# Seven products of quarters in the second feed-forward's gate and up blocks

## The chip, the cores and the metric

One core of a Trainium2 chip runs the whole layer in one launch. The engines that matter are TensorE (matmuls; PE in the profile, its weight loads PEld), VectorE (DVE), ScalarE (ACT), GpSimd (POOL) and SyncE (SP), whose queue issues the loads of weights. The metric is the device time of one execution in microseconds, as the median of several executions of the same program.

## The reference, cut to what matters

```
def swiglu(x, w_gate, w_up, w_down):
    return (jax.nn.silu(x @ w_gate) * (x @ w_up)) @ w_down

h = swiglu(rms_norm(x, ff1_pre_g), ff1_w_gate, ff1_w_up, ff1_w_down)
x = x + 0.5 * rms_norm(h, ff1_post_g)
...  # mixer: differential attention heads and state-space groups, then w_out
x = x + rms_norm(mixed, mix_post_g)
h = swiglu(rms_norm(x, ff2_pre_g), ff2_w_gate, ff2_w_up, ff2_w_down)
x = x + 0.5 * rms_norm(h, ff2_post_g)
```

There are 512 tokens of 1024 channels; the hidden width of both feed-forwards is 2816, that is 22 blocks of 128. All inputs and the output are float32.

## The kernel before, in words

Every float32 product is computed as three matmuls of rounded numbers (fp32r): each operand is split into a high part (a cast on ACT) and a low part (a subtraction on DVE), and `mm3` multiplies high by high, high by low and low by high into the same PSUM tile. So a block of 128 hidden channels times 512 tokens over 1024 channels is 8 x 3 = 24 matmuls of 512 columns.

`Normed` (line 208) holds the normed input, transposed to channels by tokens, as two `hi` and two `lo` tiles. Its method `tile(t)` treats 128 tokens: sums of squares on ACT, scaling on DVE into `xs`, four transposes of each half on PE into `ps_xn`, and from there the cast and the subtraction.

The second feed-forward begins with `gate_up_start` (line 348): blocks 0 and 1 of gate and up, four products in the four `acc` banks of PSUM. `halves` runs them in two passes, tokens 0 to 255 and then tokens 256 to 511, with matmuls of 256 columns; between the products of the first pass it lets in the transposes of token tiles 2 and 3. Their weights are split ahead (`w_lead`, the low part on POOL). `gate_up` (line 353) then does blocks 0 and 1's `finish` and goes through blocks 2 to 21: for gate and up each, one weight block is loaded (512 KB, SP queue), split (`wh` by ACT, line 154; `wl` by DVE, line 155), and multiplied (`ps_gu`, lines 188 to 190). `finish` makes silu of the gate on ACT (`sg`, L361), multiplies on DVE (`hf`, L363), and splits the product at once into high and low `h` (L365 and L366). `out_block` (line 316) multiplies h by the down weights in two passes of 512 output channels, with h as the stationary operand.

Buffers come from pools with a fixed number of slots: 3 for raw weights, 4 for each of `wh` and `wl`, 15 pages of 8 KB a partition in the heap, 2 for rows of gains, 6 for `scratch`, and 8 PSUM banks (4 `acc`, 2 `m`, 2 `sc`). An instruction that needs a slot waits for the last reader of an older tile. Inside the block `with tc.manual_schedule(engines={PE})` TensorE's order is the order of the program; the order of the other engines is made at build time by a planner that simulates the program and lets each engine take the first ready instruction in program order. `after(ins)` puts the instructions of ins's engine that are traced inside it behind ins. `behind` (line 354) keeps the splits of the next weights on ACT and DVE behind the last norm work of the input.

Of the kernel before, what the change touches and what calls it, by code (L numbers as in the profile page):

```python
# [8 lines left out]
F32 = mybir.dt.float32  # L9
F32R = mybir.dt.float32r  # L10
# [3 lines left out]
ALU = mybir.AluOpType  # L14
# [28 lines left out]
HEAD_PADS = (2.05, 0.85, 1.0, 0.6)  # L43
GLU_COST = (0.8, 0.65, 1.0)
GT = "m"


@with_exitstack
def hybrid_layer(
# [21 lines left out]
    def page(shape, dtype=F32, name="page"):  # L71
        return heap.tile(shape, dtype, tag="page", name=name)
# [6 lines left out]
    def scratch(shape, dtype=F32, name="scratch"):  # L79
        return tmp.tile(shape, dtype, tag="scratch", name=name)  # L80
# [70 lines left out]

    def split(raw, wh, wl, eng=dve, rows=None):
        if rows is None:
            act.copy(wh, raw)  # L154
# [51 lines left out]
        return s  # L206

    class Normed:
        def __init__(self, gain, g=None):
            self.g = g if g is not None else gain_row(gain, DM, "pre_g")  # L210
            self.hi = [page([P, 4, SEQ], F32R, "xn_hi") for _ in range(2)]
            self.lo = [page([P, 4, SEQ], F32R, "xn_lo") for _ in range(2)]

        def tile(self, t, hold=(), pads=()):
            xt = x_sb[t]
            ss = [sum_sq(xt[:, h * 512:(h + 1) * 512], 1.0 / 32, f"pre{h}") for h in range(2)]
            self.last_sq = sum_sq.ins
            with after(*hold[0:1]):
                r = rsqrt_of(ss, EPS, "pre")
            xs = []  # L220
            for h in range(2):
                xs.append(scratch([P, 512], F32, "xs"))
                cs = slice(h * 512, (h + 1) * 512)
                with after(*hold[1:]):
                    self.last = dve.scalar_tensor_tensor(xs[h], xt[:, cs], r, self.g[:, cs], ALU.mult, ALU.mult).ins
            yield
            for h in range(2):
                ps = bank("m" if h else "sc", "ps_xn")
                for k in range(4):
# [7 lines left out]
                self.lo_ins = dve.tensor_tensor(self.lo[h][:, :, t * P:(t + 1) * P], pv, hi.bitcast(F32),  # L237
                                                ALU.subtract).ins

        def get(self, k, a=0, b=SEQ):  # L240
            return self.hi[k // 4][:, k % 4, a:b], self.lo[k // 4][:, k % 4, a:b]
# [67 lines left out]
    def drain(gen):  # L309
        while True:  # L310
            try:
                next(gen)
            except StopIteration as e:
                return e.value

    def out_block(lhs, w, nf, last, gain, half, finished, hooks={}, order0=None, tags0=("acc",) * NT, gains_of=None):
# [19 lines left out]
        steps = row_steps(lhs, w, nf, 0, order0 or outer(nf, 4), done0, hooks, tags0, gains_of=gains_of)  # L336
# [5 lines left out]
        yield drain(row_steps(lhs, w, nf, 512, outer(nf, last), done1, hooks, norm_at=norm_at, gains_of=gains_of))  # L342
# [10 lines left out]
    def gate_up(xn, first, w_gate, w_up, tick=None):  # L353
# [17 lines left out]
        for f in range(lead, NF):  # L371
# [8 lines left out]
            if f >= 3:  # L380
                behind.clear()
        return lambda f: (h[f // 2][:, f % 2, 0, :], h[f // 2][:, f % 2, 1, :])


    rows_left = []
# [688 lines left out]
    for _ in background:  # L1074
        pass

    def next_norm(gain, lead):
        box = {}

        def start():  # L1080
            box["n"] = Normed(gain)
            box["w"] = lead()

        return box, start, lambda t: box["n"].tile(t)
# [43 lines left out]
            for _ in range((1, 4, 1)[GLU_ORDER[:n].count(c)]):  # L1128
                yield next(parts[int(c)])

    box, start, fin = next_norm(ff2_pre_g, lambda: gate_up_lead(ff2_w_gate, ff2_w_up))
# [13 lines left out]
    with tc.manual_schedule(engines={mybir.EngineType.PE}):  # L1145
# [46 lines left out]
```

## Time and profile before

| | us |
|---|---|
| median of 3 runs | 957.99 (957.38 to 958.18) |
| profiled execution, its own time | 962.16 |
| its span, first to last instruction | 960.4 |
| PE busy in the span | 946.3 (99%) |
| DVE busy | 470.5 (49%) |
| ACT busy | 333.0 (35%) |
| POOL busy | 78.0 (8%) |

Matmuls are pipelined, so a busy PE is not PE at its peak: the pace is read from the starts of successive matmuls. The granted clock of TensorE is 1.00 in all 40 slices but the last stretch, which is 2.4 GHz.

### The profile page before, as it was taken

How to read it: one execution, taken by the hardware profiler on the slowest of the kernel's cores; microseconds unless marked ns; L12 is line 12 of the kernel's file. 1: busy time of each engine (PE TensorE's matmuls, PEld its weight loads, DVE VectorE, ACT ScalarE, POOL GpSimd, SP SyncE). 2: the span in 40 equal slices, each digit the busy share in tenths (PEclk: the TensorE clock that was granted, in tenths of full speed). 3: DMA queues.
4: the chain of work that ended last, by engine and by line, in shares of the span. 5: the costliest groups of instructions: out<-in, count | busy, mean ns of one | idle time of the engine just before them, and what ended most of it. 6: DMA issues, size and time to landing. Idle time of an engine off the chain costs nothing.

```text
span 960.4 us, 12657 instructions
## 1 busy us (share of the span) xinstructions
PE 946.3 (99%) x4956; PEld 785.7 (82%) x4956; DVE 470.5 (49%) x919; ACT 333.0 (35%) x558; POOL 78.0 (8%) x157
## 2 busy tenths in 40 slices
PE   9999999999999999999999999999999999999997
PEld 5988878888888888988777778988888888888886
DVE  5599987433322324739578658333333333322323
ACT  5422333232311233523657565323223232222311
POOL 2100000000000031110122334000000000000000
PEclk9999999999999999999999999999999999999999
DMA  6636453533223264753612142333333333323212
GB/s 197 182 94 171 126 161 114 156 88 105 93 90 109 88 214 158 176 132 100 111 44 89 44 125 75 109 93 104 88 110 88 99 99 90 108 88 105 93 44 88
DMA packets 145981, 106.85 MB, mean 111 GB/s; under 512 B 15585, under 2 KB 126721, under 8 KB 145154
## 3 DMA queue, kind: packets, MB, share of 16 engines
q1 hardware_dynamic: 143776, 100.93, 35.9%
q0 software_dynamic: 992, 3.02, 1.0%
q10 hardware_dynamic: 1154, 2.10, 0.6%
q8 instruction: 39, 0.64, 0.3%
q14 instruction: 20, 0.16, 0.1%
HBM read 97.15 MB, written 8.88 MB: 110 GB/s over the span
## 4 chain that ended last, share of the span: by engine, by line
PE 47%; DVE 3%; DMA 2%; issue 1%; ACT 1%; POOL 1%; DVEq 0%; POOLq 0%; SPq 0%; ACTq 0%
PE ps_gu L188 8%; PE ps_gu L189 8%; PE ps_gu L190 8%; PE acc L188 5%; PE acc L190 5%; PE acc L189 5%; DMA om<-om_d 1%; PE ps_o L958 1%; DMA mm<-kd 1%; DMA raw<-in_ff_w_gate_dram 1%; PE ps_sc L929 0%; PE ps_k L188 0%; PE ps_y L817 0%; PE ps_k L190 0%; PE ps_xn L230 0%
## 5 line engine op out<-in xcount | busy, mean ns | idle before, releaser
L154 ACT CAST wh<-raw 128x1024 fp32r<-128x1024 f32 x146 | 153.2, 1052 | 468.7 <-issue 165.3
L155 DVE TENSOR_TENSOR wl<-raw,wh 128x1024 fp32r<-128x1024 f32 x146 | 180.4, 1239 | 276.1 <-ACT wh L154 253.8
L188 PE MATMUL ps_gu<-xn_hi,wh 128*128 128x512 f32 (+1 forms) x696 | 265.4, 382 | 0.0
L189 PE MATMUL ps_gu<-xn_lo,wh 128*128 128x512 f32 (+1 forms) x696 | 265.0, 381 | 0.0
L190 PE MATMUL ps_gu<-xn_hi,wl 128*128 128x512 f32 (+1 forms) x696 | 264.9, 381 | 0.0
L190 PEld LDWEIGHTS ps_gu<-xn_hi,wl 128*128 128x128 f32 x696 | 130.8, 188 | 25.3 <-issue 0.2
L188 PEld LDWEIGHTS ps_gu<-xn_hi,wh 128*128 128x128 f32 x696 | 130.7, 188 | 25.3 <-issue 0.6
L189 PEld LDWEIGHTS ps_gu<-xn_lo,wh 128*128 128x128 f32 x696 | 130.9, 188 | 24.5
L189 PE MATMUL acc<-wl,h 128*128 128x512 f32 x352 | 136.8, 389 | 0.0
L188 PE MATMUL acc<-wh,h 128*128 128x512 f32 x352 | 136.7, 389 | 0.0
L190 PE MATMUL acc<-wh,h 128*128 128x512 f32 x352 | 136.3, 389 | 0.0
L363 DVE TENSOR_TENSOR hf<-sg,ps_gu 128x512 f32<-128x512 f32 x44 | 30.3, 688 | 109.1 <-PE ps_gu L190 108.3
L190 PEld LDWEIGHTS acc<-wh,h 128*128 128x128 f32 x352 | 66.1, 188 | 13.8
L189 PEld LDWEIGHTS acc<-wl,h 128*128 128x128 f32 x352 | 66.1, 188 | 13.7
L188 PEld LDWEIGHTS acc<-wh,h 128*128 128x128 f32 x352 | 66.1, 188 | 13.5
L325 POOL TENSOR_SCALAR ss<-ss_post 128x1 f32<-128x1 f32 x12 | 2.6, 213 | 544.2 <-ACT junk_post L205 544.2
L365 ACT CAST h<-hf 128x512 fp32r<-128x512 f32 x44 | 27.3, 621 | 11.2 <-DVE hf L363 10.5
L366 DVE TENSOR_TENSOR h<-hf,h 128x512 fp32r<-128x512 f32 x44 | 30.2, 686 | 1.4 <-ACT h L365 1.4
L205 ACT ACTIVATE junk_post<-acc 128x512 bf16<-128x512 f32 x24 | 14.3, 594 | 37.8 <-PE acc L190 37.5
L361 ACT ACTIVATE sg<-ps_gu 128x512 f32<-128x512 f32 x44 | 25.9, 589 | 1.8 <-PE ps_gu L190 1.8
L492 DVE TENSOR_TENSOR pslots<-itca,a 128x128 f32<-128x128 f32 (+2 forms) x48 | 20.2, 466 | 8.6 <-DMA kd<-pslots 8.2
L155 POOL TENSOR_TENSOR w_lead<-raw,w_lead 128x1024 fp32r<-128x1024 f32 x8 | 19.6, 2455 | 21.1 <-ACT w_lead L154 21.1
(284 smaller groups left out, 1130.8 us busy)
## 6 DMA issues: line engine op xcount, KB each, us to landing
raw<-in_ff_w_gate_dram SPq DMA_DIRECT2D x44, 512.0 KB, 3.9
raw<-in_ff_w_up_dram SPq DMA_DIRECT2D x44, 512.0 KB, 4.0
raw<-in_ff_w_down_dram SPq DMA_DIRECT2D x44, 512.0 KB, 3.3
raw<-in_w_in_dram SPq DMA_DIRECT2D x16, 512.0 KB, 4.6
raw<-in_w_out_dram SPq DMA_DIRECT2D x8, 512.0 KB, 3.3
im_d<-itca SPq DMA_DIRECT2D x4, 512.0 KB, 3.4
om_d<-taps SPq DMA_DIRECT2D x4, 512.0 KB, 3.9
im<-im_d SPq DMA_DIRECT2D x2, 1024.0 KB, 10.0
```

What stands on the lines that cost most here:

```text
L154: act.copy(wh, raw)
L155: eng.tensor_tensor(wl, raw, wh.bitcast(F32), ALU.subtract)
L188: pe.matmul(ps, a[0], b[0], start=start, stop=False)
L189: pe.matmul(ps, a[0], b[1], start=False, stop=False)
L190: last_mm[:] = [pe.matmul(ps, a[1], b[0], start=False, stop=stop).ins]
L205: sum_sq.ins = act.activation(into, src, AF.Square, scale=scale, accum_out=s).ins
L361: act.activation(sg, ps_g, AF.Silu)
L363: dve.tensor_tensor(hf, sg, ps_u, ALU.mult)
L365: act.copy(hi, hf)
L366: dve.tensor_tensor(lo, hf, hi.bitcast(F32), ALU.subtract)
L492: dve.tensor_tensor(t[ri], a, by, ALU.mult)
L958: pe.matmul(po[:, os], at[:, kb * P:(kb + 1) * P], A.v[:, kb, h * VD:(h + 1) * VD], start=(kb == 0), stop=(kb == i), skip_group_check=True)
```

## The change

For gate and up each, blocks f and f + 10 (f from 2 to 11) are computed together as a product of 2 x 2 quarters: a pair's 256 hidden channels, the 1024 input channels and the 512 tokens are all halved, and eight products of quarters become seven (a Winograd form of Strassen's scheme). A quarter product has 4 steps over channels of 3 matmuls of 256 columns. `Normed` keeps a third, unrounded copy of the transposed input (`raw`, copied by ACT), and `combine` makes four combinations of its quarters on DVE, each split into high and low. `prepared` loads the two weight blocks of a job, splits the first as it is (parts 1 and 2), makes four combinations of quarters in place on DVE, and splits what results (parts 6 and 3, part 7, parts 5 and 4). A `Job` owns two PSUM banks, each of them holding two quarters of 256 columns. Between the products, ACT copies partial sums out of PSUM (`p1`, `u2`, `p5`, `u3`) and DVE adds them to other quarters in PSUM. There are 20 jobs. h is kept whole (`keep`), and `Held` splits it when the down products need it, once in each of the two passes.

The products are now traced inside the block in which PE's order is the program's.

```diff
     class Normed:
-        def __init__(self, gain, g=None):
+        def __init__(self, gain, g=None, keep=False):
+            self.raw = [page([P, 4, SEQ], F32, "xn_raw") for _ in range(2)] if keep else None
+            self.late = []
...
+            if t >= 2:
+                self.flush()
...
                 self.hi_ins = act.copy(hi, pv).ins
+                if self.raw:
+                    self.late.append(lambda o=self.raw[h][:, :, t * P:(t + 1) * P], i=pv: act.copy(o, i))
...
+        def combine(self):
+            self.flush()
+            (b11, b12), (b21, b22) = ([r[:, :, 0:256], r[:, :, 256:512]] for r in self.raw)
+            out, self.cut_ins = {}, []
+            def parts(name, v):
+                both = page([P, 2, 4, 256], F32R, "xt")
+                self.cut_ins.append(act.copy(both[:, 0], v).ins)
+                dve.tensor_tensor(both[:, 1], v, both[:, 0].bitcast(F32), ALU.subtract)
+                out[name] = both[:, 0], both[:, 1]
+            dve.tensor_tensor(b11, b12, b11, ALU.subtract)
+            dve.tensor_tensor(b12, b22, b12, ALU.subtract)
+            dve.tensor_tensor(b22, b22, b11, ALU.subtract)
+            parts(6, b22)
+            parts(7, b12)
+            parts(5, b11)
+            dve.tensor_tensor(b21, b21, b22, ALU.subtract)
+            parts(4, b21)
...
+    class Held:
+        def __call__(self, f):
+            if f // 2 not in self.cut:
+                self.cut[f // 2] = both = page([P, 2, 2, SEQ], F32R, "h_cut")
+                for n in range(2):
+                    hv = self.at[f // 2 * 2 + n]
+                    act.copy(both[:, n, 0], hv)
+                    dve.tensor_tensor(both[:, n, 1], hv, both[:, n, 0].bitcast(F32), ALU.subtract)
...
+    def gate_up_seven(xn, first_two, w_gate, w_up):
...
+        def prepared(w, f0, f1):
+            def raw():
+                turn[0] += 1
+                if RAWPAGE and turn[0] % 4 == 0:
+                    return gains.tile([P, KD, P], F32, tag="gain", name="raw")
+                return ring.tile([P, KD, P], F32, tag="raw", name="raw", bufs=3)
...
+            by[1], by[2] = parts(ra)
+            s3 = scratch([P, 4, P], F32, "s3")
+            dve.tensor_tensor(s3, a11, a21, ALU.subtract)
+            dve.tensor_tensor(a21, a21, a22, ALU.add)
+            dve.tensor_tensor(a11, a21, a11, ALU.subtract)
+            dve.tensor_tensor(a12, a12, a11, ALU.subtract)
+            by[6], by[3] = parts(ra)
+            h3, l3 = (scratch([P, 4, P], F32R, f"s3{c}") for c in "hl")
+            split(s3, h3, l3)
+            by[7] = h3, l3
+            by[5], by[4] = parts(rb)
...
+            def product(self, m):
+                ps = {1: self.c11, 2: self.c11, 3: self.c12, 6: self.c12, 4: self.c21, 7: self.c21, 5: self.c22}[m]
+                (wh, wl), (xh, xl) = self.by[m], xt[m]
+                for k in range(4):
+                    for i, (a, b) in enumerate(((wh, xh), (wh, xl), (wl, xh))):
+                        pe.matmul(ps, a[:, k], b[:, k], start=(m in (1, 7) and k == i == 0), ...
...
+        job, nxt = Job(0), None
+        xt.update(xn.combine())
+        with after(xn.cut_ins[CUT], *job.s_ins):
+            for f in range(lead):
+                keep(f, gate(first_two[2 * f][0]), first_two[2 * f + 1][0])
+        first(job)      # product 1 into c11; ACT copies it to p1
+        second(job)     # product 6 into c12; DVE adds p1; ACT copies the sum to u2
+        for n, (w, f0, f1) in enumerate(jobs):
+            nxt = Job(n + 1) if n + 1 < len(jobs) else None
+            job.product(7)
+            job.product(5)
+            add(job.c21, job.c21, u2)
+            act.copy(u3, job.c21)
+            act.copy(p5, job.c22)
+            add(job.c22, job.c22, u3)
+            if nxt:
+                first(nxt)
...
+            job.product(2)
+            job.product(3)
+            add(job.c12, job.c12, p5)
+            job.product(4)
+            if nxt:
+                second(nxt)
+            if n % 2 == 0:
+                sgs = [gate(b) for b in job.banks]
+            else:
+                for f, sg, b in zip((f0, f1), sgs, job.banks):
+                    keep(f, sg, b)
...
-    lhs = gate_up(box["n"], lhs, ff2_w_gate, ff2_w_up)
+        lhs = gate_up_seven(box["n"], lhs, ff2_w_gate, ff2_w_up)
```

A job's seven products run on PE as 7, 5, (1 of the next job), 2, 3, 4, (6 of the next job).

## Rows read from the trace of the kernel before

**Rows 1.** The page, part 1: busy us, share of the span, instructions.
```profile
PE 946.3 (99%) x4956; PEld 785.7 (82%) x4956; DVE 470.5 (49%) x919; ACT 333.0 (35%) x558; POOL 78.0 (8%) x157
```

**Rows 2.** Stretches: lead blocks' products, blocks 2 to 21, first pass of the down products.
```profile
core 0: us, PE busy (x) PEld busy (x) DVE busy (x) ACT busy (x) POOL busy (x), PEclk, DMA share, GB/s
592.01:616.77 24.76, 24.76 (x209) 24.75 (x208) 14.19 (x20) 11.24 (x19) 2.15 (x4) 1.00 0.36 107
616.77:834.40 217.63, 217.63 (x962) 180.25 (x961) 73.70 (x79) 62.14 (x79) 0.00 (x0) 1.00 0.32 95
834.40:896.00 61.60, 61.60 (x273) 51.05 (x272) 17.45 (x17) 15.71 (x21) 0.85 (x4) 1.00 0.26 86
```

**Rows 3.** Timeline of PE, start and duration in us, at three stage borders.
```profile
605.25 0.28 PE L188 MATMUL ps_gu<-xn_hi,w_lead 128*128 128x256 f32 x1
...
616.77 0.40 PE L188 MATMUL ps_gu<-xn_hi,wh 128*128 128x512 f32 x1
...
834.40 0.39 PE L188 MATMUL acc<-wh,h 128*128 128x512 f32 x1
```

**Rows 4.** Waits from 617 to 835 us: us in total, times, longest.
```profile
DVE wl L155 <- ACT wh L154: 73.2, 20, 4.2
DVE hf L363 <- PE ps_gu L190: 71.1, 21, 3.7
```

**Rows 5.** Groups by line and form, blocks 2 to 21: busy us, mean ns.
```profile
L155 DVE TENSOR_TENSOR wl<-raw,wh 128x1024 fp32r<-128x1024 f32 x39 | 47.8, 1226 | 75.9 <-ACT wh L154 73.2
L154 ACT CAST wh<-raw 128x1024 fp32r<-128x1024 f32 x39 | 41.1, 1054 | 150.6 <-PE ps_gu L189 76.7 <-issue 69.8 <-PE ps_gu L190 4.1
L366 DVE TENSOR_TENSOR h<-hf,h 128x512 fp32r<-128x512 f32 x20 | 13.7, 686 | 0.7 <-ACT h L365 0.7
L365 ACT CAST h<-hf 128x512 fp32r<-128x512 f32 x20 | 12.4, 622 | 3.1 <-DVE hf L363 3.1
```

**Rows 6.** Groups by line and form, whole run: shapes the change uses elsewhere.
```profile
L494 DVE TENSOR_TENSOR itca<-pslots 128x256 f32<-128x256 f32 x8 | 3.4, 420 | 0.0
...
L361 ACT ACTIVATE sg<-ps_gu 128x512 f32<-128x512 f32 x44 | 25.9, 589 | 1.8 <-PE ps_gu L190 1.8
...
L951 ACT COPY att<-ps_at 128x256 f32<-128x256 f32 x4 | 1.5, 372 | 0.9 <-PE ps_at L949 0.9
...
L189 PE MATMUL ps_gu<-xn_lo,w_lead 128*128 128x256 f32 x64 | 18.1, 283 | 0.0
...
L929 PE MATMUL ps_sc<-qk 128*128 128x256 f32 x16 | 5.7, 359 | 0.0
```

**Rows 7.** Timeline of DVE under the lead blocks' products; xN is a run.
```profile
592.72 1.40 DVE L225 SCALAR_TENSOR_TENSOR xs<-x,rinv_pre,pre_g 128x512 f32<-128x512 f32 x2
...
598.89 1.41 DVE L225 SCALAR_TENSOR_TENSOR xs<-x,rinv_pre,pre_g 128x512 f32<-128x512 f32 x2 [0.66 <-POOL rinv_pre L199]
600.22 3.49 DVE L155 TENSOR_TENSOR wl<-raw,wh 128x1024 fp32r<-128x1024 f32 x3
603.63 1.28 DVE L237 TENSOR_TENSOR xn_lo<-ps_xn,xn_hi 128x512 fp32r<-128x512 f32 x2
```

**Rows 8.** Timeline of PE: first transposes of token tiles 2 and 3.
```profile
594.89 0.27 PE L230 MATMUL ps_xn<-ident,xs 128*128 128x128 f32 x1
...
601.51 0.27 PE L230 MATMUL ps_xn<-ident,xs 128*128 128x128 f32 x1
```

**Rows 9.** Timeline of ACT under the lead blocks' products.
```profile
602.15 1.08 ACT L236 CAST xn_hi<-ps_xn 128x512 fp32r<-128x512 f32 x2 [1.33 <-PE ps_xn L230]
...
606.69 1.28 ACT L361 ACT_TABLE_LOAD   x1
```

**Rows 10.** Timelines of SP's queue and of POOL: loads of weights and gains.
```profile
581.70 0.37 SPq L174 DMA_DIRECT2D raw<-in_ff_w_gate_dram  x1
601.47 0.37 SPq L174 DMA_DIRECT2D raw<-in_ff_w_up_dram  x1
...
598.80 0.64 POOL L144 DMA_DIRECT2D post_g<-in_ff_post_g_dram  x1
```

More of the change, by code (lines that the diff above doesn't have):

```diff
@@ L45 @@
 GT = "m"
+LATE1 = False
+OWN = True
+NXT = False
+CUT = 3
+SINS = True
+RAWPAGE = True
 @with_exitstack
@@ L153, in split @@
         if rows is None:
-            act.copy(wh, raw)
+            split.ins = act.copy(wh, raw).ins
             eng.tensor_tensor(wl, raw, wh.bitcast(F32), ALU.subtract)
@@ L382, in gate_up, with __init__, fresh @@
         return lambda f: (h[f // 2][:, f % 2, 0, :], h[f // 2][:, f % 2, 1, :])
+    class Held:
+        def __init__(self, at):
+            self.at, self.cut, self.used = at, {}, False
+        def fresh(self):
+            if self.used:
+                return Held(self.at)
+            self.used = True
+            return self
+        def __call__(self, f):
[5 more added lines that the diff above has]
+                    dve.tensor_tensor(both[:, n, 1], hv, both[:, n, 0].bitcast(F32), ALU.subtract)
+            both = self.cut[f // 2]
+            return both[:, f % 2, 0, :], both[:, f % 2, 1, :]
@@ new lines, in gate_up_seven, with keep, gate, parts @@
+    def gate_up_seven(xn, first_two, w_gate, w_up):
+        lead = len(first_two) // 2
+        at, free = {}, []
+        def keep(f, sg, ps):
+            if not free:
+                pg = page([P, 4, SEQ], F32, "h")
+                free.extend(pg[:, j] for j in range(4))
+            at[f] = free.pop(0)
+            dve.tensor_tensor(at[f], sg, ps, ALU.mult)
+        def gate(ps):
+            sg = scratch([P, SEQ], F32, "sg")
+            act.activation(sg, ps, AF.Silu)
+            return sg
+        n = (NF - lead) // 2
+        jobs = [(w, lead + p, lead + p + n) for p in range(n) for w in (w_gate, w_up)]
+        xt, turn = {}, [0, 0]
+        def prepared(w, f0, f1):
[4 more added lines that the diff above has]
+                return ring.tile([P, KD, P], F32, tag="raw", name="raw", bufs=3)
+            ra, rb = raw(), raw()
+            for r, f in ((ra, f0), (rb, f1)):
+                sp.dma_start(out=r, in_=w[0, :, f * P:(f + 1) * P].rearrange("(k p) c -> p k c", p=P))
+            a11, a12, a21, a22 = ra[:, 0:4], ra[:, 4:8], rb[:, 0:4], rb[:, 4:8]
+            def parts(v):
+                turn[1] += 1
+                if OWN and turn[1] % 5 == 0:
+                    both = page([P, 2, KD, P], F32R, "w_own")
+                    wh, wl = both[:, 0], both[:, 1]
+                else:
+                    wh = ring.tile([P, KD, P], F32R, tag="wh", name="wh")
+                    wl = ring.tile([P, KD, P], F32R, tag="wl", name="wl")
+                split(v, wh, wl)
+                return [(wh[:, k:k + 4], wl[:, k:k + 4]) for k in (0, 4)]
+            by = {}
+            by[1], by[2] = parts(ra)
[7 more added lines that the diff above has]
+            split(s3, h3, l3)
+            by["ins"] = split.ins
+            by[7] = h3, l3
+            by[5], by[4] = parts(rb)
+            return by
+        class Job:
+            def __init__(self, n):
+                self.by = prepared(*jobs[n])
+                self.s_ins = [self.by["ins"]] if SINS else []
+                tags = ("m", "sc") if n % 2 else ("acc", "acc")
+                self.banks = [bank(t, "ps_gu") for t in tags]
+                u, v = self.banks
+                self.c11, self.c12, self.c21, self.c22 = u[:, 0:256], u[:, 256:512], v[:, 0:256], v[:, 256:512]
+            def product(self, m):
[3 more added lines that the diff above has]
+                    for i, (a, b) in enumerate(((wh, xh), (wh, xl), (wl, xh))):
+                        pe.matmul(ps, a[:, k], b[:, k], start=(m in (1, 7) and k == i == 0), stop=(k == 3 and i == 2),
+                                  skip_group_check=True)
+        def add(o, v, w):
+            dve.tensor_tensor(o, v, w, ALU.add)
+        aside = gains.tile([P, 4, 256], F32, tag="gain", name="aside")
+        p1, u2, p5, u3 = (aside[:, j] for j in range(4))
+        def first(job):
+            job.product(1)
+            act.copy(p1, job.c11)
+        def second(job):
+            job.product(6)
+            add(job.c12, job.c12, p1)
+            act.copy(u2, job.c12)
+        job, nxt = Job(0), None
[5 more added lines that the diff above has]
+        second(job)
+        sgs = None
+        for n, (w, f0, f1) in enumerate(jobs):
+            if not NXT:
+                nxt = Job(n + 1) if n + 1 < len(jobs) else None
[5 more added lines that the diff above has]
+            add(job.c22, job.c22, u3)
+            if NXT:
+                nxt = Job(n + 1) if n + 1 < len(jobs) else None
+            if nxt and not LATE1:
+                first(nxt)
+            if not nxt:
+                held = Held(at)
+                held(0)
+            job.product(2)
+            if nxt and LATE1:
+                first(nxt)
+            job.product(3)
[5 more added lines that the diff above has]
+                sgs = [gate(b) for b in job.banks]
+            else:
+                for f, sg, b in zip((f0, f1), sgs, job.banks):
+                    keep(f, sg, b)
+            job = nxt
+        return held
```

18 lines of the change are left out of this document (13 added, 5 removed).

## The prediction

> **What bounds the kernel now.** I read the page's busy shares first: PE is busy 99% of the span, DVE 49%, ACT 35% [rows 1]. The shares by stretch come next. Blocks 2 to 21, the ones that change, take 217.63 us with PE never idle, DVE busy for 73.70 and ACT for 62.14 [rows 2]. The waits there are DVE waiting for ACT's cast and ACT and DVE waiting for PE's products, never PE for them [rows 4]. So in this stretch a matmul less is time less, and vector work costs nothing until it no longer fits beside PE. "Busy" doesn't give PE's pace; the starts do. Forty block products of 24 matmuls are 960 matmuls between 616.77 and 834.40 [rows 3]: 217.63 / 960 = 226.7 ns for 512 columns. The second pass of `halves`, 4 products of 24 matmuls of 256 columns without a transpose between, runs from 605.25 to 616.77 [rows 3]: 11.52 us / 96 = 120.0 ns. Doubling the columns adds 106.7 ns, and 13.3 ns a matmul don't shrink with them. The granted clock is 1.00 in both, the level of 2.4 GHz [rows 2].
>
> **PE's part of the change.** Twenty jobs of 7 products of 12 matmuls are 1680 matmuls of 256 columns: 1680 x 120.0 = 201.6 us, against 217.6 now. That is 16.0 us less, 7% and not the eighth that seven for eight would give, because each narrower matmul pays the 13.3 ns too. No transposes lie among them. A bound from the other side is the same width in the scores of the attention, where a matmul lasts 359 ns in place of 283 [rows 6], beside transposes and bf16 work; break-even is already at 217.63 / 1680 = 129.5 ns, 9.5 over the row. I take 120.0, the row with the same operands, order and half-bank output.
> The Trainium skill (TensorE: Matmul & The Clock Gate, Back-to-back issue gap) states a warm gap of columns / 2.4 plus about 2.5 ns; by it 512 columns would take 215.8 ns and 256 columns 109.2, and the saving would be an estimated 23.7 us. The two paces here are 10.9 and 10.8 ns above that, so I stay with the rows.
>
> **DVE's part.** Per job: three parts of 1024 columns at 1226 ns; four combinations and the low part of s3, all 512 columns, and on average one multiplication by the gate, six at 686 [rows 5]; four additions of 256 columns at 420 [rows 6]. That is 3.68 + 4.12 + 1.68 = 9.48 us per job, where PE needs 84 x 120 = 10.08. Durations in isolation overcount: three subtractions of 1024 in a row took 3.49 us, so a further one costs 1.13, and two of 512 took 1.28, so a further one 0.60 [rows 7]. With 0.34 for 256 columns (420 less the same 0.08, an estimate) the sum is 3.39 + 3.60 + 1.36 = 8.35 us. DVE goes from a third of the stretch to 83 to 94%. ACT has three casts at 1.054 and one at 0.622 [rows 5], four copies at 0.372 and a silu at 0.589 [rows 6]: 5.9 us per job, 58%. PE stays the bound if DVE is not kept waiting; its margin is 0.6 to 1.7 us a job.
>
> **The new waits.** PE's order is fixed, so a product that comes late stops all behind it. I counted the room of each in products of 12 x 0.120 = 1.44 us. Products 6, 2 and 3 need copies that were due at least three products earlier. The narrow one is product 4: its quarter needs u2 added (DVE 0.42), and the sum copied (ACT 0.37). The room is products 5, 1, 2 and 3.
> The Trainium skill (PSUM — Partial Sum Buffer, PSUM bank collisions raise a hardware error) says that two engines may not touch one bank in the same partitions at once, different columns or not, so their accesses have to be ordered by bank. It speaks against a layout with two quarters in a bank. No row of before shows a matmul into a bank that is being read.
> If the accesses are ordered by bank, the chain is longer: after product 5 an addition, two copies and another addition, 0.42 + 0.37 + 0.37 + 0.42 = 1.58 us, and the room is 3 products, 4.3 us. What remains, 2.7 us, has to hold the queueing on DVE and ACT, where a part of 1.23 us or a cast of 1.05 [rows 5] may be in front. DVE and ACT run their queues in order, and the next job's preparation is traced ahead of these additions, so it goes first where it is ready. Bounds for PE's lost time per job: 0 where the planner slips the additions in between, 3.2 us where the whole preparation after part 1 (five of 512, two of 1024: 5.9 us) stands in front (1.58 + 5.9 - 4.3). I take 0.1 us, near the lower end, because slots ration the preparation: a part's slot comes free only when a product of an earlier job is done, so preparation comes in pieces with gaps for a 0.42 us addition. Twenty jobs: 2 us.
>
> **Buffers and loads.** The four `wh` slots serve four of every five parts, and five parts are 1.67 jobs, so each may be held for 16.8 us; the longest hold, parts 1 and 2, is nine products and 2.3 us of splitting, 15.3. Loads stay at 1 MB per job, 104 GB/s against 95 [rows 2]. The gain slot lent to every fourth raw block is first free after the pre-gains' last use at 600.3 [rows 7]; loads queued behind it on SP lose nothing, since that queue already stood from 581.70 to 601.47 [rows 10]. The post-gains' load on POOL, now at 598.80 [rows 10], moves to the stage's end; nothing queues behind it that matters, and its first reader comes after 18 of 22 down blocks, 18 x 12 x 0.2267 = 49 us on. Free.
>
> **Ahead of the stretch.** The first job's splits no longer stand behind the norm (`behind` is not used), and their raw blocks have been loaded long before 592. ACT and DVE will fill gaps with them, and a 1.23 us part may stand before `xs` of tile 2 or 3. The slack: `xs` of tile 2 ends at 594.12, its transposes start at 594.89; tile 3, 600.30 and 601.51 [rows 7, 8]. Between 0 and 2.5 us (two parts, each just begun, eating the smaller slack once); I take 0.7. The raw copies on ACT, eight of 512 columns, fit its idle time.
> At the border DVE owes, from 600.3: job 0's preparation (3 x 1.13 + 5 x 0.60 = 6.4), tile 3's low parts 1.28, `combine` with 8 x 1.13 = 9.0, and two multiplications 1.2: 17.9 us, to 618.2 if without gaps. Product 1 needs only the first silu, which stands behind the fourth cut on ACT and a table load of 1.28 [rows 9], about 615.5, before 616.8. Product 6, due at 618.2, needs the first cut, product 7 the second, and the later ones follow at the rate at which DVE makes them. Job 0 also waits once for p1's copy between products 1 and 6 if banks are ordered, 0.5 us. So 0 to 4 us; I take 1.5.
>
> **The down products.** h's split moves: 20 casts and 20 subtractions leave the stretch, 44 of each enter the down passes. In the first pass DVE grows from 17.45 by 22 x 0.69 to 32.6 of 61.6 us, ACT from 15.71 to 29.4 [rows 2, 5]. One pair of blocks is 24 matmuls, 5.4 us, against 2.6 us of DVE; without that cover each pair would cost 1.4 us. The last job makes the first pair's cut early, and the h it finishes last is needed 9 blocks later. I cost this at nothing, at most 1 us.
>
> **Sum.** -16.0 + 0.7 + 1.5 + 2.0 = -11.8. The profiled execution (962.16) would become 950.4; it stands 4.2 us above the median of the runs, and a difference carries over: 957.99 - 11.8 = 946.2, so 946.
>
> **Rivals.**
> A, DVE becomes the bound (chance 0.18). For it: the isolated sum of 9.48 us, and a hand-over from ACT before each part. Against it: back-to-back rows at 8.35. With another 1 us of waits a job takes 10.5 us, the stretch 210, and with the 2.2 us of the border the time is 957.99 - 7.6 + 2.2 = 952.6; 950 to 956.
> B, the other side (0.14): product 4 waits in the same bank behind preparation in DVE's queue. It decides from 0.69 us per job on, the (16.0 - 2.2) / 20 that would be saved. If the full 3.2 us come in one job of three, 21 us are lost: 957.99 - 13.8 + 21 = 965. For it: DVE's share and the order in which the program is traced; against it: the rationing by slots.
> C, the change doesn't do what it says (0.04): narrow matmuls at another place's pace. At 129.5 ns nothing is left and the border makes it 960. Against it: 96 matmuls in a row at 120.0.
> D, the narrow matmuls shed part of the 13.3 ns in the new layout (0.04): with half of it, 113.3 ns, the stretch is 190.4 us and the time 957.99 - 27.2 + 4.2 = 935. For it is nothing here but that the quarter's stationary and moving tiles lie otherwise; against it, the two paces of [rows 3]. The page's rule above would be this case.
> The forecast, PE-bound with small losses, has 0.60 and its own range 942 to 951.
>
> **Chances and range.** About 0.2%, 1.9 us, is what can be told from no change. Faster holds the forecast, D and nearly all of A: 0.81; slower B and part of C: 0.14; the same, 0.05. The lower end is 941.5, all 16.0 us and little else; the upper end 957 takes in A and leaves out most of B.
>
> **What would show it.** In the stretch 140 products at 1.44 us, 201.6 us from the first matmul after the lead blocks to the first down product, plus gaps; DVE 165 to 190 us busy there, ACT near 117. If B holds, PE is idle before product 4 and the releaser is an addition on DVE. If A holds, PE waits for `wl`. If C, the starts are over 120 ns apart without idle time. The prediction is wrong if PE idles more than 0.7 us a job, or if the lead blocks' 24.76 us grow by over 3.

## The result, and the profile after

The changed kernel's median is 949.75 us (946.32 to 951.32, 4 runs), beside 958.09 (957.38 to 960.57, 4 runs) of the kernel before on the same chip. The ratio is 0.9895 [0.9873, 0.9917]; the medians alone make 0.9913. Measured again on another chip (the first experiment), 949.2 stood against 960.64. The profiled execution took 949.65 us (span 947.9), the one before 962.16 (span 960.4).

The page's busy shares, which answer to [rows 1]:
```profile
PE 932.0 (98%) x5676; PEld 807.4 (85%) x5676; DVE 602.7 (64%) x1149; ACT 407.1 (43%) x712; POOL 81.8 (9%) x157
```
PE has 720 more instructions (1680 narrow ones in place of 960 wide ones) and 14.3 us less work. DVE gained 132 us and ACT 74, and PE is still the engine that is always busy.

The same three stretches as [rows 2]: lead blocks, blocks 2 to 21 in pairs, first pass of the down products. Columns: us, busy us of PE, weight loads, DVE, ACT and POOL with instructions, granted clock, DMA share, GB/s.
```profile
591.80:616.70 24.90, 24.90 (x209) 24.69 (x207) 23.69 (x31) 16.01 (x26) 1.64 (x3) 1.00 0.23 64
616.70:821.90 205.20, 203.33 (x1670) 201.66 (x1671) 169.38 (x255) 107.69 (x182) 0.64 (x1) 1.00 0.36 103
821.90:883.00 61.10, 61.10 (x282) 51.08 (x281) 35.22 (x49) 30.92 (x50) 1.33 (x2) 1.00 0.29 95
```
In the middle stretch DVE grew from 73.70 to 169.38 us and ACT from 62.14 to 107.69, as PE shrank. DVE now is at 83%: close, but not the bound.

The borders on PE's timeline (start, duration, what came ahead of it in brackets), as [rows 3]:
```profile
616.42 0.28 PE L196 MATMUL ps_gu<-xn_hi,w_lead 128*128 128x256 f32 x1
617.26 0.39 PE L522 MATMUL ps_gu<-xn_hi,wh 128*128 128x256 f32 x1 [0.56 <-ACT sg L462]
...
618.67 0.28 PE L522 MATMUL ps_gu<-xn_hi,wl 128*128 128x256 f32 x1
619.41 0.51 PE L522 MATMUL ps_gu<-xt,wh 128*128 128x256 f32 x2 [0.46 <-ACT aside L533]
...
820.04 0.39 PE L196 MATMUL acc<-wh,h_cut 128*128 128x512 f32 x1
820.27 0.28 PE L522 MATMUL ps_gu<-xn_hi,wh 128*128 128x256 f32 x1
...
824.58 0.40 PE L194 MATMUL acc<-wh,h_cut 128*128 128x512 f32 x1
...
941.34 0.39 PE L196 MATMUL acc<-wh,h_cut 128*128 128x512 f32 x1
```
The pair products can begin at 616.54 (616.42 and one pace of 0.12) and their last ends at 824.58. In the last job 12 wide down matmuls are slipped in ahead of 820.27; they are worth 12 x 0.2267 = 2.72 us and belong to the next stage. So the stretch costs 824.58 - 616.54 - 2.72 = 205.32 us where it cost 217.63: 12.31 less. What follows, to the last matmul's start, is 941.34 - 824.58 + 2.72 = 119.48 us. Before, the last matmul was
```profile
953.86 0.39 PE L190 MATMUL acc<-wh,h 128*128 128x512 f32 x1
```
and the same piece took 953.86 - 834.40 = 119.46 us: nothing changed there. The lead blocks take 24.82 (from 591.72 to 616.54), against 24.76. The gain lies in one stretch.

What PE waits for there, from the view of waits (total us, times, longest), where [rows 4] had no wait of PE:
```profile
PE ps_gu L522 <- ACT sg L462: 0.6, 1, 0.6
PE ps_gu L522 <- DVE ps_gu L526: 0.5, 1, 0.5
PE ps_gu L522 <- ACT aside L533: 0.5, 1, 0.5
PE ps_gu L522 <- DVE wl L161: 0.3, 1, 0.3
```
Four single waits of at most 0.6 us in 20 jobs. A wait costs PE a little more than its own length: 618.67 to 619.41 is 0.74 us where the pace is 0.12, so 0.62 were lost for a wait of 0.46.

### The profile page after: what moved, and what is told of

It is laid out like the page before. It is cut to its first block, busy times and chain, and to the rows that moved or that the text cites. A ratio compares the mean times of both kernels' runs of the same rounds, so it can differ in the third digit from the quotient of the medians.

```text
span 947.9 us, 14507 instructions
## 1 busy us (share of the span) xinstructions
PE 932.0 (98%) x5676; PEld 807.4 (85%) x5676; DVE 602.7 (64%) x1149; ACT 407.1 (43%) x712; POOL 81.8 (9%) x157
## 4 chain that ended last, share of the span: by engine, by line
PE 87%; DVE 6%; ACT 3%; DMA 2%; issue 1%; POOL 0%; DVEq 0%; POOLq 0%; ACTq 0%
PE ps_gu L522 17%; PE acc L194 10%; PE acc L196 10%; PE acc L195 10%; PE ps_gu L194 9%; PE ps_gu L196 9%; PE ps_gu L195 9%; DVE wl L161 1%; DMA raw<-in_ff_w_up_dram 1%; PE ps_o L1154 1%; PE ps_y L1013 1%; PE ps_warm L126 1%; PE ps_u L195 1%; PE ps_q L194 1%; PE ps_u L196 1%
## 5 line engine op out<-in xcount | busy, mean ns | idle before, releaser
L194 PE MATMUL ps_gu<-xn_hi,wh 128*128 128x512 f32 (+1 forms) x376 | 140.9, 376 | 0.0
L195 PE MATMUL ps_gu<-xn_lo,wh 128*128 128x512 f32 (+1 forms) x376 | 140.5, 374 | 0.0
L196 PE MATMUL ps_gu<-xn_hi,wl 128*128 128x512 f32 (+1 forms) x376 | 140.5, 374 | 0.0
L196 PEld LDWEIGHTS ps_gu<-xn_hi,wl 128*128 128x128 f32 x376 | 70.7, 188 | 12.8 <-issue 0.2
L522 PE MATMUL ps_gu<-xt,wh 128*128 128x256 f32 x384 | 71.0, 284 | 0.9 <-DVE ps_gu L526 0.5
L195 PE MATMUL acc<-wl,h_cut 128*128 128x512 f32 x176 | 68.5, 389 | 0.0
L195 PE MATMUL acc<-wl,h 128*128 128x512 f32 x176 | 68.3, 389 | 0.0
L194 PE MATMUL acc<-wh,h 128*128 128x512 f32 x176 | 68.2, 389 | 0.0
L196 PE MATMUL acc<-wh,h 128*128 128x512 f32 x176 | 68.2, 389 | 0.0
L194 PE MATMUL acc<-wh,h_cut 128*128 128x512 f32 x176 | 67.8, 389 | 0.0
L196 PE MATMUL acc<-wh,h_cut 128*128 128x512 f32 x176 | 67.5, 389 | 0.0
L196 PEld LDWEIGHTS acc<-wh,h 128*128 128x128 f32 x176 | 33.0, 188 | 6.9
```

The source lines that it names most:

```text
L194: pe.matmul(ps, a[0], b[0], start=start, stop=False)
L195: pe.matmul(ps, a[0], b[1], start=False, stop=False)
L196: last_mm[:] = [pe.matmul(ps, a[1], b[0], start=False, stop=stop).ins]
L522: pe.matmul(ps, a[:, k], b[:, k], start=(m in (1, 7) and k == i == 0), stop=(k == 3 and i == 2), skip_group_check=True)
```

## The experiments

A ratio is to the kernel before, run beside it on the same chip. "The stretch" of a kernel with the seven products is from the start of the last lead matmul to the first down product behind the last pair product, the slipped ones left in: 824.58 - 616.42 = 208.16 us in the first profile. (In experiments 2 and 3 it starts with the first product of block 2, as in [rows 3].)

**1. The changed kernel once more** (no edit), more runs.

> The changed kernel once more, nothing edited, timed against the kernel before in five rounds. Theory 1 (the sum of the prediction holds, -11.8 us; the profiled executions differ by 12.5 us of span): the ratio is 0.987 to 0.988, 946 us against 958, and the smaller difference of the first medians (8.3 us) was the scatter of single executions. Rival (a loss outside the profiled stretches that single profiles miss): the ratio is 0.991, 8 to 9 us. The trace of this execution should repeat the stretch of the seven products within 0.5 us of 205.2; if executions differ in time, the difference should lie outside it.

949.2 us against 960.64, ratio 0.9892 [0.9876, 0.9908]. The interval reaches down to theory 1's values and ends just under the rival's 0.991; the ratio itself lies between the two, at 10 to 11 us. The stretch in its profile is 208.74 us, 0.58 longer than in the first profile, where at most 0.5 was expected. Some of what scatters between executions lies elsewhere: over the profiles of all the runs here, the first matmul of split operands (`ps_gu<-xn_hi,wh` of the first feed-forward) starts between 11.8 and 16.4 us after the span's start, before any of the changed work.

**2. Narrow matmuls without the change** (blocks 2 to 21 of the kernel before, each product in two passes of 256 columns):
```diff
-                col_mm(ps, col_weights(w, f * P), xn, 0, SEQ)
+                wts = col_weights(w, f * P)
+                for a in (0, 256) if narrow else (0,):
+                    col_mm(ps, wts, xn, a, a + 256 if narrow else SEQ)
```


> The kernel before, with blocks 2 to 21 of the second feed-forward multiplied in two passes of 256 columns in place of one of 512: 1920 matmuls of 256 columns, no arithmetic saved. Theory 1 (13.3 ns a matmul don't shrink with the columns): 1920 x 120.0 = 230.4 us in place of 217.6, so 12.8 us slower, about 971, ratio 1.013; this is the part of the eighth that the seven products lose. Rival (the cost goes with the columns, and the seven products lose their time to waits): no change within 2 us.

973.89 us, ratio 1.0149 [1.013, 1.0167]. The stretch, with the columns as above:
```profile
616.07:846.47 230.40, 230.40 (x1923) 230.40 (x1922) 73.69 (x79) 61.34 (x79) 0.00 (x0) 1.00 0.30 90
```
It starts with a gate product at 616.07 and ends with the first down product at 846.47, so 1920 matmuls take 230.40 us: 120.0 ns each, without one idle moment. The pace that the prediction took from 96 matmuls holds for 1920; splitting the columns costs 12.77 us. Seven eighths of that, 11.2 us, is what the change pays of the 27.2 us that an eighth of the stretch is worth; 16.0 are left.

**3. h kept whole, without the seven products** (kernel before, h split when the down products use it):
```diff
-        steps = row_steps(lhs, w, nf, 0, ...)
+        steps = row_steps(fresh(), w, nf, 0, ...)
...
-    lhs = gate_up(box["n"], lhs, ff2_w_gate, ff2_w_up)
+    lhs = gate_up(box["n"], lhs, ff2_w_gate, ff2_w_up, whole=True)
```


> The kernel before, with the second part of the change alone: h of the second feed-forward is kept whole and split when the down products use it, in each of the two passes; products as before. Theory 1 (hidden beside PE): within 1 us of before, DVE near 33 of 61 us in the first down pass, no PE wait there. Rival (the splits come late for the down products, or free time on DVE and ACT in the gate and up stretch is worth something): over 2 us slower, or over 2 us faster.

960.31 us, ratio 1.0001 [0.9987, 1.0015]. The same two stretches:
```profile
615.21:832.83 217.62, 217.62 (x962) 180.19 (x961) 68.90 (x72) 58.25 (x74) 0.00 (x0) 1.00 0.32 92
832.83:894.43 61.60, 61.60 (x273) 51.03 (x272) 27.54 (x36) 24.40 (x39) 1.33 (x2) 1.00 0.29 94
```
DVE's 17.45 us in the down pass [rows 2] became 27.54 (33 had been expected) and ACT's 15.71 became 24.40, and both stretches last what they lasted. The split costs nothing where PE covers it. All of the gain is the seven products'.

**4. Product 4's room taken away** (product 4 ahead of product 3, so two products and not three lie between product 5 and it and the order of the sums is kept):
```diff
+            job.product(4)
             job.product(3)
             add(job.c12, job.c12, p5)
-            job.product(4)
```


> The changed kernel with product 4 one place earlier in each job: 7, 5, 1 of the next, 2, 4, 3, 6 of the next. All work is the same; the room between product 5 and product 4 shrinks from three products, 4.32 us, to two, 2.88. Theory 1 (product 4 waits for all four accesses to its bank, the later addition to the other quarter included): in the trace of the changed kernel that addition ends 1.9 to 4.9 us after product 5, median 3.1; what exceeds 2.88 sums to about 11 us over 20 jobs, so the run is 8 to 13 us slower than the changed kernel, and the waits on PE are put down to the additions on DVE. Rival (product 4 waits only for its own quarter, the first addition and its copy, over a product earlier): under 3 us slower.

958.21 us, ratio 0.9974 [0.9959, 0.9989]; the stretch and the down products took 9.7 us more than in experiment 1. PE's main wait, then one case of it on PE, on DVE and on ACT:
```profile
PE ps_gu L522 <- DVE ps_gu L526: 8.3, 7, 1.6
```
```profile
691.15 0.39 PE L522 MATMUL ps_gu<-xt,wh 128*128 128x256 f32 x1 [1.63 <-DVE ps_gu L526]
```
```profile
688.21 0.43 DVE L526 TENSOR_TENSOR ps_gu<-ps_gu,aside 128x256 f32<-128x256 f32 x1
689.53 1.23 DVE L161 TENSOR_TENSOR wl<-raw,wh 128x1024 fp32r<-128x1024 f32 x1 [0.89 <-ACT wh L160]
690.67 0.42 DVE L526 TENSOR_TENSOR ps_gu<-ps_gu,aside 128x256 f32<-128x256 f32 x1
```
```profile
688.44 1.05 ACT L160 CAST wh<-raw 128x1024 fp32r<-128x1024 f32 x1
689.39 0.38 ACT L554 COPY aside<-ps_gu 128x256 f32<-128x256 f32 x1
```
Between the two additions on DVE (688.21 and 690.67) lie two copies on ACT, of u3 (L554) and right behind it of p5, and on each engine a piece of the next job's preparation got in front: a cast of 1.05 us, then its low part of 1.23. Product 4 starts as soon as the second addition is done. This is rival B of the prediction, and one product of 1.44 us is what keeps it away.

**5. Is it the order in which the preparation is traced?** (experiment 4, and the next job's preparation traced after the additions):
```diff
-NXT = False
+NXT = True
```


> The run with product 4 one place earlier, and in it the next job's preparation traced after the additions and copies of this job's bank instead of ahead of them, so that the additions go first in DVE's queue. Theory 1 (the additions are late because preparation stands in front of them, not because the chain itself is long: 1.58 us of work against 2.88 of room): the 9 us lost by the earlier product 4 come back by at least two thirds, to within 3 us of the changed kernel, unless the preparation itself becomes late and PE waits for weight parts. Rival (the chain's own hand-overs are what is long): it stays 8 to 10 us slower than the changed kernel.

956.61 us, ratio 0.9979 [0.9958, 0.9999]; the stretch 218.16 us, against 219.14 in experiment 4. One microsecond came back of ten. PE still waited 7.3 us in 7 places for the additions. DVE's order was nearly the same; it seems that the planner puts first what it finds ready first, wherever it is traced. My theory that trace order decides fell.

**6. The order forced** (experiment 5, and all of the preparation after its first part held behind the second addition, the next p1 copy behind p5's):
```diff
             by[1], by[2] = parts(ra)
+            with after(*hold):      # and all that follows in the preparation
...
-            act.copy(p1, job.c11)
+            with after(*hold[:1]):
+                act.copy(p1, job.c11)
```


> The run with product 4 one place earlier (which lost 9.7 us in the two stretches against the changed kernel's second profile), with two orders now written out: the next job's p1 copy on ACT behind this job's p5 copy, and all of the next job's preparation after part 1 behind this job's second addition on DVE and p5 copy on ACT. (Tracing the preparation later had left DVE's order the same, additions behind it.) Theory 1 (what is late for product 4 are queue places: a part or a cast in front of the additions, the next p1 copy in front of the u3 copy; the chain alone is 1.58 us): waits before product 4 fall to the last job's and a few tenths, 6 to 9 us come back, unless product 6 then waits for its weight part; in that case the PE waits name the low parts. Rival (the bank's hand-overs themselves take over 2.9 us): no more than 2 us come back.

1006.51 us, ratio 1.0502 [1.0478, 1.0526]. The second addition now ended 1.85 us after product 5 in 18 of 20 jobs, and product 4, with 2.88 us of room, waited for nothing. But PE waited for the weights:
```profile
PE ps_gu L523 <- ACT wh L160: 14.9, 15, 2.2
PE ps_gu L523 <- DVE wl L161: 11.0, 14, 0.9
```
and its clock over the stretch (columns as above) was below 1.00:
```profile
614.85:880.64 265.79, 226.96 (x1705) 217.68 (x1703) 177.08 (x257) 111.30 (x183) 0.64 (x1) 0.96 0.28 82
```
The chain is as short as it was worked out to be, and the fix lengthened the stretch by 46.65 us over experiment 4, almost five times what it cures: cast and low part of the next job alternate between ACT and DVE and need the time before the additions too. Up to 11 us of the 46.65 are clock and not wait (an estimate, 0.04 of 265.79 us).

**7. and 8. More work on DVE** (the changed kernel, and 4, then 8, maxima of 256 columns per job from the second job on, on a spare tile that nothing reads: 1.34 and 2.68 us a job on the average):
```diff
             dve.tensor_tensor(a12, a12, a11, ALU.subtract)
+            load = junk["pre"].bitcast(F32)
+            for _ in range(4 if turn[0] > 2 else 0):
+                dve.tensor_tensor(load, load, load, ALU.max)
```


> The changed kernel with four more additions of 256 columns on DVE in every job but the first (on a spare tile; nothing reads the result): 4 x 0.335 = 1.34 us a job more. In the trace of the changed kernel DVE is busy 169 of 205 us, 8.5 us a job of 10.1, so it would have 9.8. Theory 1 (PE stays the bound; losses come only where an addition is late for product 4, whose chain has a median of 1.2 us to spare): 2 to 8 us slower than the changed kernel, the waits on PE put down to additions. Rival A (DVE is the bound as soon as its isolated durations reach PE's 10.1, here 9.5 + 1.7): over 15 us slower. If nothing is lost, DVE had room to spare after all.

> The same with eight such additions a job, 2.68 us more: 11.2 us of DVE work where PE has 10.1. Theory 1 (DVE's back-to-back work then sets the pace): 19 jobs x 1.1 = 21 us slower than the changed kernel at least, 21 to 35 with the waits; DVE busy over 95% of the stretch. Rival (another engine's chain is what limits): under 15 us.

Four: 961.31 us against 958.65, ratio 1.0023 [1.0009, 1.0037]; the stretch 221.44, 12.7 more than in experiment 1. Eight: 967.68, ratio 1.0089 [1.0067, 1.011]; the stretch 230.33, 21.6 more. The last of the 76 spare maxima with four a job, then that stretch cut in two behind it, and the time behind two of the waits:
```profile
717.81 0.41 DVE L502 TENSOR_TENSOR junk_pre<-junk_pre 128x256 f32<-128x256 f32 x1
```
```profile
615.33:718.00 102.67, 93.27 (x751) 91.65 (x749) 99.79 (x183) 50.98 (x84) 0.00 (x0) 0.98 0.30 86
718.00:836.77 118.77, 116.99 (x948) 115.72 (x947) 94.56 (x143) 61.91 (x103) 0.64 (x1) 0.99 0.35 104
698.00:701.50 3.50, 3.50 (x19) 3.50 (x18) 3.40 (x8) 1.47 (x3) 0.00 (x0) 0.51 0.75 213
773.00:776.00 3.00, 2.96 (x15) 2.66 (x14) 3.00 (x4) 0.23 (x1) 0.00 (x0) 0.52 0.32 92
```
and the stretch with eight:
```profile
614.00:843.00 229.00, 209.97 (x1693) 205.39 (x1694) 216.96 (x399) 111.48 (x184) 0.64 (x1) 1.00 0.32 93
```
PE's main wait with four:
```profile
PE ps_gu L525 <- DVE ps_gu L529: 6.5, 5, 1.9
```
With eight, DVE is busy 95% of the stretch and sets the pace; without the six more down matmuls that slipped in, the stretch grew by 20.2 us, a little under the 21 that were expected at least. With four the whole gain is gone already: 25 us of work added, 12.7 us lost. That is more than theory 1 had and less than the rival's. But the load was not spread as the expectation had it. Nothing holds the spare maxima back, so they ran as early as DVE had room, 11 of them ahead of the stretch and the last at 717.81. Up to there DVE was busy for 99.79 of 102.67 us, 97%, and about 11 of the 12.7 us were lost (job 9 begins 106.85 us after the stretch's start, and 95.97 in the first profile of the changed kernel); behind it DVE is at 80%, where the changed kernel has 81% from 718 us on. So this run doesn't show what 1.34 us more in every job would do; it shows, as the one with eight does, that a full DVE sets the pace. PE's waits come to 11.2 us where they were 1.9, most of them for additions (L529). Part of the loss is clock: after PE had stood for 1.89 us, the granted clock was 0.51, the 1.2 GHz level, for 3.5 us, and 19 matmuls went where 29 would have at 120 ns; after a stand of 1.74 us it fell so once more, from 773 to 776 us.

**9. The border's waits removed** (a small silu early for the table, and job 0's product 7 between 1 and 6):
```diff
+        with after(xn.hi_ins):
+            act.activation(tiny(1, "silu"), x_sb[3][:, 0:1], AF.Silu)
...
         first(job)
+        job.product(7)
         second(job)
...
-            job.product(7)
+            if n:
+                job.product(7)
```


> The changed kernel with the border between the lead blocks and the first job eased in two places: a small silu ahead of the cuts brings ACT's table load forward, and in the first job product 7 is put between products 1 and 6, so that PE has work while p1 is copied out of the bank that product 6 writes. Theory 1 (the 1.5 us at the border are these two waits, 0.82 and 0.72 us, the second because the copy reads the same bank): both waits vanish in the trace, 1.4 us in all, 0.15%; too little to be told in the times. Rival (DVE's backlog is what holds the border, and the waits move to the next product): the stretch from the first product to the first down product is no shorter.

946.24 us, ratio 0.9871 [0.9847, 0.9895]. The border and PE's waits:
```profile
615.97 0.28 PE L196 MATMUL ps_gu<-xn_hi,w_lead 128*128 128x256 f32 x1
616.29 0.39 PE L522 MATMUL ps_gu<-xn_hi,wh 128*128 128x256 f32 x1
...
617.71 0.28 PE L522 MATMUL ps_gu<-xn_hi,wl 128*128 128x256 f32 x1
617.83 0.40 PE L522 MATMUL ps_gu<-xt,s3h 128*128 128x256 f32 x2
```
```profile
PE ps_gu L522 <- DVE ps_gu L526: 0.9, 2, 0.5
PE ps_gu L522 <- DVE wl L161: 0.3, 1, 0.3
```
Both waits of the border are gone but for 0.2 us at 616.29, and 617.71 to 617.83 is the plain pace. The stretch is 208.03 us, against 208.16 and 208.74 of the changed kernel: of the 1.3 us gained at the border, 0.6 to 1.2 came back as later waits, the 0.9 us for additions among them. So theory 1 holds for the two waits, and the rival for most of the time. The intervals of the two ratios overlap, so this edit is not shown to be faster.

**10. Border and forced order together**, with product 4's room as in the change (the edits of 6 and 9):

> The changed kernel with the eased border and with the written-out order of the run before, product 4 in its old place. Theory 1: the stretch loses its 1.4 us at the border and about 1.5 of the 2 us of waits inside, so 2 to 3 us less than the changed kernel, near 946 where that has 949, ratio to before 0.985 to 0.988. Rival (the forced order makes the weight parts late): waits on low parts appear, and it is not faster than the changed kernel, or slower by several us.

1027.26 us, ratio 1.0694 [1.0665, 1.0723]. The two additions on DVE, PE's waits, and the clock over the stretch:
```profile
702.50 0.43 DVE L527 TENSOR_TENSOR ps_gu<-ps_gu,aside 128x256 f32<-128x256 f32 x1 [3.65 <-PE ps_gu L523]
703.65 0.43 DVE L527 TENSOR_TENSOR ps_gu<-ps_gu,aside 128x256 f32<-128x256 f32 x1 [0.71 <-ACT aside L561]
```
```profile
PE ps_gu L523 <- ACT wh L160: 22.4, 15, 2.1
PE ps_gu L523 <- DVE wl L161: 11.7, 14, 1.9
```
```profile
612.23:894.35 282.12, 234.59 (x1694) 225.87 (x1693) 177.67 (x259) 113.39 (x185) 0.64 (x1) 0.91 0.26 75
```
The rival came true: DVE stands idle for 3.65 us while the work that PE needs next is held back. The stretch is 73 us longer than in experiment 1; up to 25 of them are clock (an estimate, 0.09 of 282.12 us). The first addition's start to the second's end is 703.65 + 0.43 - 702.50 = 1.58 us, to the hundredth the chain that the prediction added up. A chain that already fits gains nothing from being made first.

**11. Fewer buffers** (no page of its own for every fifth part, no gain slot for raw blocks):
```diff
-OWN = True
+OWN = False
-RAWPAGE = True
+RAWPAGE = False
```


> The changed kernel without its extra buffers: no heap page for every fifth weight part and no gain slot for every fourth raw block, so 4 slots for 3 parts a job and 3 for 2 raw blocks. A slot may then be held 1.33 jobs, 13.4 us, where parts 1 and 2 are held about 15.3 and the three parts of a job 12.5 on average. Theory 1 (slots are rationed but suffice on the average): preparation loses its lead, 3 to 12 us slower than the changed kernel, waits on PE for low parts and additions. Rival (buffers are far from binding): within 1 us.

950.56 us, ratio 0.9909 [0.9889, 0.993]; stretch and down products 2.8 us longer than in experiment 1, a little under the 3 to 12 expected. PE waits 2.2 us for casts and low parts, where it waited 0.3. The buffers matter less than the prediction's count (15.3 of 16.8 us) let one think.

**12. Only the p1 copy held** (experiment 9, and the next job's p1 copy behind p5's on ACT):
```diff
-                first(nxt)
+                first(nxt, hold)     # hold: the p5 copy
```


> The changed kernel with the eased border and one order on ACT written out: the next job's p1 copy behind this job's p5 copy. In the changed kernel the p1 copy, which waits for product 1, stands in front of the u3 copy in most jobs, so that the second addition ends 3.1 us after product 5. Only this one copy is moved; preparation keeps its place. Theory 1 (that copy is part of the chain's length): where nothing else stands in front, the second addition ends under 2.7 us after product 5, the waits on additions inside the stretch (0.9 us with the eased border) shrink or stay, and the time is that of the eased border within 1 us. Rival (any written-out order upsets the planner's, as forcing the preparation did, 64 us and more): slower by over 3 us.

951.08 us, ratio 0.9904 [0.9887, 0.992]; the stretch 211.21, 3 us longer than in experiment 9. The second addition ends 2.75 us after product 5 in the median, where it was 3.1 in the changed kernel, and still PE waits 2.1 us for additions and 2.0 for low parts, against 0.9 and 0.3. A shorter chain in the median, and no gain from it: PE waits where the chain is longest, and in four jobs the second addition ended over 4.32 us after product 5 (4.33 to 5.16), in experiment 9 in two (4.80 and 4.92). Theory 1's time, within 1 us of experiment 9, missed; the stretch shows the rival's loss of over 3 us.

## Why the prediction was right

**PE's pace: right.** 1680 matmuls at 120.0 ns were to take 201.6 us. The stretch took 205.32, and the distances between PE's starts that exceed the pace add up to 3.7 us, so 201.6 again; experiment 2 shows the pace by itself. The rule of the Trainium skill (TensorE: Matmul & The Clock Gate, Back-to-back issue gap), 109.2 ns for 256 columns, which the page gives for the gap of a single matmul and not for a stream with its weight loads, would have made an estimated 183.5 us for the 1680; the 230.40 us of experiment 2's 1920 stand against it here. Rivals C and D fall with the same row.

**The border: right, 1.5 us expected and 1.54 measured.** It has the two parts that were named. The first silu stands behind the cuts and the table load on ACT, and product 6 waits for p1's copy:
```profile
611.40 3.89 ACT L264 CAST xt<-xn_raw 128x1024 fp32r<-128x1024 f32 x4 [4.00 <-DVE xn_raw L270]
615.31 1.28 ACT L462 ACT_TABLE_LOAD   x1
616.61 1.09 ACT L462 ACTIVATE sg<-ps_gu 128x512 f32<-128x512 f32 x2
618.98 0.37 ACT L533 COPY aside<-ps_gu 128x256 f32<-128x256 f32 x1 [1.29 <-PE ps_gu L522]
```
The silu came 1.1 us later than the 615.5 that I had worked out. Start to start, PE lost 617.26 - 616.42 - 0.12 = 0.72 and 0.62 there, and 0.10 more at the start after each.

**Inside the stretch: the sum right, 2.0 us expected and 2.2 measured (3.7 less 1.5), but only 0.7 of it at product 4.** The prediction put all of it on product 4. Start to start, product 4 lost 0.7 us, all in job 13; product 6 of jobs 2, 4 and 14 lost 1.1 us, waiting for the low part of its own weights; the rest is smaller pieces. The second profile (experiment 1) has 1.0 and 1.1. The prediction had looked at product 6 only for copies and named a wait for `wl` only as the sign of rival A, so the late low part was a term that it put at nothing, and that the sums agree is partly luck. In 20 jobs the second addition ends 1.85 to 4.9 us after product 5, in the median 3.1, and the room is 4.32; it ran over clearly once, in job 13. PE there, with product 6 of job 14 behind it, then DVE:
```profile
759.79 0.28 PE L522 MATMUL ps_gu<-xn_hi,wl 128*128 128x256 f32 x1
760.53 0.50 PE L522 MATMUL ps_gu<-xt,wh 128*128 128x256 f32 x2 [0.46 <-DVE ps_gu L526]
...
762.72 0.39 PE L522 MATMUL ps_gu<-xt,wl 128*128 128x256 f32 x1 [0.26 <-DVE wl L161]
```
```profile
757.38 0.43 DVE L526 TENSOR_TENSOR ps_gu<-ps_gu,aside 128x256 f32<-128x256 f32 x1
757.71 1.22 DVE L161 TENSOR_TENSOR w_own<-raw,w_own 128x1024 fp32r<-128x1024 f32 x1
758.84 0.68 DVE L497 TENSOR_TENSOR raw<-raw 128x512 f32<-128x512 f32 x1
759.45 0.69 DVE L499 TENSOR_TENSOR raw<-raw 128x512 f32<-128x512 f32 x1
760.05 0.76 DVE L526 TENSOR_TENSOR ps_gu<-ps_gu,aside 128x256 f32<-128x256 f32 x2
```
A low part and two combinations of the next job stood between the two additions. Product 4 writes the bank's first half (c21); what it waited for is the addition into the other half (c22), which ended at about 760.45. So in this program the accesses are ordered by the whole bank and not by the quarter. That is what the Trainium skill (PSUM — Partial Sum Buffer, PSUM bank collisions raise a hardware error) asks of a program, and the border's product 6 shows it too: it writes c12 and waits for the copy out of c11. Without that order the chain would be the first addition, over at 757.81, and the copy of its sum on ACT (L554, 0.37 us from 757.84), over at 758.21 and 1.7 us ahead of the product.

**DVE and rival A: right, with less margin than it seemed.** The sum came to 169.38 / 20 = 8.5 us a job, at the back-to-back end of 8.35 to 9.48; ACT's 107.69 are 5.4 a job where 5.9 were worked out. ACT thus stayed under the 117 us that were named as a sign. Rival A's mechanism is real: where spare work brought DVE to 97% of 103 us, about 11 us were lost (experiment 7). Its sign, PE waiting for `wl`, is there in the 1.1 us above.

**Ahead of the stretch: 0.7 expected, next to nothing measured** (24.82 against 24.76 us). DVE is busy for 23.69 of 24.90 us there, and the pieces of preparation fell into gaps; what came late by it is counted at the border.

**Down products: right.** 119.48 against 119.46 us with DVE at 35.22 us and ACT at 30.92 in the first pass, and experiment 3 shows the split's cost alone as 0. The prediction's "2.6 us of DVE" for a pair of blocks is a slip: two casts of 0.62 on ACT and two subtractions of 0.69 on DVE make 2.6, and DVE's share is 1.4. It changes nothing in the sum.

**Sum.** -16.0 + 0 + 1.5 + 2.2 = -12.3, where -16.0 + 0.7 + 1.5 + 2.0 = -11.8 was predicted. The rest of the distance from 946.0 to 949.75 is not in the terms: the four executions scatter by 5 us and their medians differ by 8.3, those of experiment 1 by 11.4, the profiles by 12.5. In the two profiles the first matmul of split operands starts at the same 16.43 us, so the start has no part in their 12.5.

**What stays open.** Why the time before that matmul scatters by 4.6 us between executions was not studied, nor whether it is what sets the 8.3 apart from the 11.4. A bank's two quarters are also one tile of the program, and nothing here tells an order by bank from an order by tile. And nothing here shows how PE would do with quarters in banks of their own, since that was not tried.

## What to carry to other kernels

Work out the pace of a narrower operation from starts in a stretch without gaps, and count what does not shrink with it: here 13.3 ns a matmul turned 12.5% of the stretch into 7%, and two paces in the trace told it in advance. A chain across engines needs room in the bounding engine's fixed order, counted with the queues it passes through and with all users of a bank; one product of slack was worth 9.7 us. Before forcing an order, look whether the wait that it removes is larger than the one that it moves.

## What the runs showed of the hardware

The clock fell after some short stands of PE and not after others: in experiment 7 a wait of 1.89 us was followed by 3.5 us at 0.51, while in experiment 8 waits of up to 2.3 us left the stretch at 1.00, and with many short waits the mean over the stretch sank to 0.96 in experiment 6 and 0.91 in experiment 10. The two falls of experiment 7 had DMA shares of 0.75 and 0.32; whether the DMA has a part in them isn't shown.
